# Layer 0's attention scores: tiles of one head and 128 queries, with high and low parts stacked in 128 rows

## The chip, the core and the metric

The kernel runs on one core of one Trainium2 chip. The metric is device time in microseconds (us), the median of several executions. The engines named below are TensorE (PE; its weight loads are shown as PEld), VectorE (DVE), ScalarE (ACT), GpSimd (POOL) and SyncE (SP), which here only issues DMAs.

## The reference, cut to what matters

Two layers over 256 tokens of width 1024. Layer 0 mixes tokens by dilated causal window attention, layer 1 by gated linear attention, each followed by a gated convolutional feed-forward block; all are modulated by the conditioning vector. The change is in layer 0 alone:

```python
A_CONFIGS = ((128, 1), (512, 4), (2048, 16))      # window, dilation: three groups
A_HEADS = 16;  A_HEAD_DIM = 64

s = jnp.einsum('bnqrhe,bnkrhe->bnrhqk', qb, kk) + bias      # per group
s = jnp.where(mask, s, NEG_INF)
m = jnp.max(s, axis=-1, keepdims=True);  p = jnp.exp(s - m);  den = jnp.sum(p, axis=-1)
o = einsum(p, v) / den;  lse = m + log(den)
...
wts = jax.nn.softmax(jnp.stack(lses), axis=0)               # over the three groups
o = jnp.sum(wts[..., None] * jnp.stack(outs), axis=0)
```

Mixing three softmaxes by the softmax of their log-sums is one softmax over the keys of all three groups together, with the group's own bias. The kernel computes it so.

## The kernel before, in words

**Precision.** A product of two float32 matrices is made of three passes in a fast float32 form (`fp32r`): each operand is split into a high part and a low remainder, and `mm3` (L196) multiplies high by high, low by high and high by low (L199, L200, L201). The casts to the high part run on ACT (L172), the subtractions for the low part on DVE (L178).

**Pairs.** Layer 0's 16 heads go in 8 pairs `u` = 0 to 7, two heads of 64 columns each. The loop is at L626. For each pair the queries and keys of the three groups `g` = 0, 1, 2 are projected (48 matmuls for each g, `pqk`), and then the values of all groups (`pv`, 48 matmuls of 384 columns). Pair 0, and the queries and keys of pair 1, come from one wide weight load (`w0`); from pair 2 on each g has its own load of 1 MB (`wqk`) and the values have two loads of 768 KB (`wv`). Loads go through 4 buffers (`raw`), split weights through 3 buffers for high parts (`whi`) and 3 for low ones (`wlo`). Between them DVE works off 96 dot products for the modulation (`ada`, L140).

**From the projection to the scores.** `evacuate` (L576) takes queries and keys out of the accumulator bank. For g = 0, whose scores need the three passes, it makes high and low parts: per head an ACT multiplication for the high part (L586) and a DVE operation for the low part (L587), then one ACT copy for the key's high part (L591) and one DVE subtraction for its low part. For g = 1, 2 it is one ACT and one DVE operation (L581) in plain float32.

**Scores.** There are four score tiles per pair, `r` = 0 to 3, of 128 rows: row 0 to 63 is the first head, 64 to 127 the second, and tile r holds the 64 queries whose token number leaves the remainder r when divided by 4. `shared` (L482) makes the 256 to 260 columns of group 0 in three 128-row matmuls on queries padded with zeros, so that the two heads don't mix; `dilated` (L488) adds two blocks of 64 columns for groups 1 and 2 with matmuls of 64 rows by 64 columns in plain float32, which the chip runs in two passes each (two records). Then, by tile: DVE adds the bias and takes the row maximum in one instruction (L510), ACT takes the exponential and its row sum (L529), DVE divides (L521, L522) and PE transposes (`turn`, L536: three 128-column transposes a tile, `t`; the copies of `t` to `pt` on ACT for even r and on DVE for odd r, L546). `outputs` (L550) multiplies with the values in matmuls of 128 rows by 64 columns (L557, L561), and ACT and DVE split the result (L568, L569).

**Order.** A scheduler orders the instructions of each engine before the run; in each engine's queue that order is fixed. `behind(...)` puts an instruction after others in that order. The scores of pair u stand after its values; the transposes of pair u-1 stand inside the projection of g = 1 of pair u (the call at L671 ahead of its last twelve matmuls, the call at L678 behind them), and the outputs of pair u-1 follow the scores of pair u. From pair 3 on the copies of `t` stand behind the last evacuation (`evacuated`, L545).

**Banks.** The accumulator has 8 banks: 2 with tag `p` (queries and keys of a g, and the values, in turn), 3 with tag `s` (scores), 3 with tag `t` (transposes, outputs, one score tile). The fourth transposed tile of a pair takes the `t` bank of the first one, so it waits for the ACT copy of that one. The projection of g = 2 takes the `p` bank of g = 0.

**Bias.** `load_bias` (L364) fetches, per pair, a tile of 128 rows by 387 columns in four small DMAs (two per head) on SP's queue, from rows that the kernel computed at its start; the tile has two buffers.

Of the kernel before, what the change touches and what calls it, by code (L numbers as in the profile page):

```python
# [11 lines left out]
F32 = mybir.dt.float32  # L12
# [45 lines left out]
def trunk(ctx: ExitStack, tc: tile.TileContext, I, out):  # L58
# [202 lines left out]
    def grouped(ap):  # L261
        return ap.rearrange("p (r i) -> p r i", r=4)
# [100 lines left out]

    def load_bias(u):  # L364

        b = att.tile([P, KEYS + 3], F32, tag="bias", name="bias")
        r = rows_d[:, :]
        for hh in range(2):  # L370
            own, at = slice(CH * hh, CH * hh + CH), r.offset + (2 * u + hh) * NROW
            nc.sync.dma_start(b[own, 2 * CH :], bass.AP(r.tensor, at, [[4, CH], [1, T + 3]]))
            nc.sync.dma_start(b[own, 0 : 2 * CH].rearrange("p (g x) -> p g x", g=2),
                              bass.AP(r.tensor, at + 512, [[1, CH], [P, 2], [1, CH]]))
        return b[:, :]


    sq = wspl.tile([P, 2048], F32, tag="wlo", name="sq").rearrange("p (k t) -> p k t", k=KT)
# [97 lines left out]
    def scores(u, q, k, v, bias):  # L476


        m = tmp.tile([P, 16], F32, tag="m", name="m")
        prob = [att.tile([P, KEYS + 3], F32, tag="prob", name="prob", bufs=4) for _ in range(4)]  # L480

        def shared(s, r):  # L482
            n = T + r + r % 2
            for i, (a, b) in enumerate(((0, 0), (1, 0), (0, 1))):
                last = mm(s[:, 0:n], q[0][a][:, r].rearrange("p a b -> p (a b)"), k[0][b][:, 0:n], start=(i == 0), stop=(i == 2))
            return last

        def dilated(s, r):  # L488
            own = slice(CH * r, CH * r + CH)
            for g in (1, 2):  # L490
                at = T + r + CH * (g - 1)
                for hh in range(2):
                    e = slice(E * hh, E * hh + E)
                    last = mm(s[e, at : at + CH], q[g][e, own], k[g][e, own], start=True, stop=True)
            return last

        for tiles in ((0, 1, 2), (3,)) if u == 0 else (range(4),):
            s = {r: bank("s", "t" if r == 3 and u else "s") for r in tiles}  # L500
# [4 lines left out]
            for r in tiles:  # L505
                with behind(last):
                    last = last_s[0] = dilated(s[r], r)
            for r in tiles:
                back = bass.AP(bias.tensor, bias.offset + KEYS - 1 + r, [bias.ap[0], [-1, KEYS + r]])
                nc.vector.tensor_tensor_reduce(  # L510
                    prob[r][:, 0 : KEYS + r], s[r][:, 0 : KEYS + r], back,
                    op0=ALU.add, op1=ALU.max, scale=1.0, scalar=-3e38, accum_out=m[:, r : r + 1],
                )
        pn = []

        def normalised():

            r = len(pn)
            f = m[:, 12 + r : 13 + r]
            pn.append(att.tile([P, KEYS], F32, tag="pn", name="pn", bufs=4))  # L520
            nc.vector.tensor_scalar(grouped(pn[r][:, 0:T]), by_residue(prob[r][:, 0:T]), f, None, op0=ALU.mult)  # L521
            norms.append(nc.vector.tensor_scalar(pn[r][:, T:KEYS], prob[r][:, T + r : KEYS + r], f, None, op0=ALU.mult))  # L522

        for hh in range(2):
            rs = slice(2 * hh, 2 * hh + 2)
            nc.vector.tensor_scalar(m[:, 4:8][:, rs], m[:, 0:4][:, rs], -1.0, None, op0=ALU.mult)
            for r in (2 * hh, 2 * hh + 1):
                c = prob[r][:, 0 : KEYS + r]
# [21 lines left out]
    def outputs(u, of, pt, *after):  # L550
        v = of[0]
        heads = [slice(E * hh, E * hh + E) for hh in range(2)]
        po = bank("po", "t")
        with behind(*after):
            for n in range(2):
                for hh, e in enumerate(heads):
                    mm(grouped(po[e, :T]), v[n][:, e], pt[:, :, P * n + E * hh : P * n + E * hh + E], start=(n == 0), stop=False)  # L557
            for r in range(4):
                for hh, e in enumerate(heads):
                    at = P * (r % 2) + P + E * hh  # L560
                    last_po[0] = mm(po[e, CH * r : CH * r + CH], v[r // 2][:, at : at + E],  # L561
                       pt[:, r, T + E * hh : T + E * hh + E], start=False, stop=(r == 3))
# [6 lines left out]
        nc.vector.tensor_tensor(lv, src, hv.bitcast(F32), op=ALU.subtract)  # L569
        o_hi.append(hi)  # L570
        o_lo.append(lo)
# [4 lines left out]
    def evacuate(q, k, g, pq, pk):  # L576

        if g:  # L580
            evacuated[:] = nc.scalar.mul(q[g], pq, 0.125), nc.vector.tensor_copy(k[g], pk)  # L581
            return evacuated[1]
        qh, ql = q[0]
        for hh in range(2):
            own = slice(E * hh, E * hh + E)
            nc.scalar.mul(qh[own, :, hh, :], grouped(pq[own]), 0.125)  # L586
            nc.vector.scalar_tensor_tensor(ql[own, :, hh, :], grouped(pq[own]), 0.125, qh[own, :, hh, :].bitcast(F32),  # L587
                                           op0=ALU.mult, op1=ALU.subtract)
        pk = in_order(pk)
        kh, kl = (as_tokens(z[:, 0:T]) for z in k[0])  # L590
        evacuated[:] = nc.scalar.copy(kh, pk), nc.vector.tensor_tensor(kl, pk, kh.bitcast(F32), op=ALU.subtract)  # L591
        return evacuated[1]

    def by_group(v, pv, n):

# [13 lines left out]
    for i in range(2):  # L609
        q_pair.append([])  # L610
        for j in range(2):
            at, n = ((112, 2 * T + 112), (0, 2 * T + 16))[j] if i == 0 else (0, 2 * T)
            z = att.tile([P, n], F32R, tag=f"q0{i}{j}", name="q", bufs=1)
            nc.gpsimd.memset(z.bitcast(F32), 0.0)
            q_pair[i].append(z[:, at : at + 2 * T].rearrange("p (r h c) -> p r h c", r=4, h=2))
            if i == 0:
                for s in range(2):
                    level[s].append(z[:, at + T * s : at + T * s + T])
# [5 lines left out]
                    nc.scalar.copy(a, b)  # L624

    for u in range(NPAIR):  # L626
        with tc.issue_after(last_load[0].ins):
            bias = load_bias(u)
        place = u % 2 if u < 4 else 1
        if u == 0:  # L630
            k_hi, k_lo = ([att.tile([P, T + 4], F32R, tag=f"k0{i}{j}", name="k", bufs=1) for j in range(2)] for i in range(2))
            for z in k_hi + k_lo:
                nc.gpsimd.memset(z[:, T:].bitcast(F32), 0.0)
        q, k = [q_pair[place]], [[k_hi[place], k_lo[place]]]
# [661 lines left out]
```

## Time and profile before

| | us |
|---|---|
| three runs | 770.27, 770.59, 772.97 |
| median | 770.59 |
| the profiled execution, first to last instruction (span) | 767.7 |
| layer 0's attention within it, about 48 to 276 | 228 |

The profile has no whole time of its own for the profiled execution; what lies around its span is taken from the runs (770.59 - 767.7 = 2.9). A row of the timeline reads: start in us from the first instruction, duration, engine, line of the kernel, operation, result <- operands, rows*columns of the array for PE, shape, and the number of merged instructions; in brackets how long the engine was idle before, and what ended that. A merged row's duration runs from the start of its first instruction to the end of its last one.

### The profile page before, as it was taken

To read this page: it belongs to the slowest core of one execution; us is meant where nothing else is said; L and a number is where in the kernel's file an instruction comes from. 1 tells how busy PE (TensorE), PEld (TensorE's weight loads), DVE (VectorE), ACT (ScalarE), POOL (GpSimd) and SP (SyncE) were. 2 spreads that over 40 slices of the span, in tenths; PEclk is the share of its full clock that TensorE was granted. 3 is DMA by queue.
4 is the path that set the end of the run, shared out by engine and by line. 5 is a ranking of instruction groups with operands and counts; after the bars stand their busy time and mean duration, and the time that the engine had idled before them with its cause. 6 is when DMAs were issued, how large, how long until landed. Compare 5 with 4: busy or idle time off the path is not lost.

```text
span 767.7 us, 15963 instructions
## 1 busy us (share of the span) xinstructions
PE 759.3 (99%) x6430; PEld 739.0 (96%) x6430; DVE 640.6 (83%) x1160; ACT 485.5 (63%) x949; POOL 13.2 (2%) x28
## 2 busy tenths in 40 slices
PE   8999999999999999999999999999999999999997
PEld 6999999999999999999999998899999999999996
DVE  6998988888888869999999778797668899998552
ACT  6477566465646568776767556745767866666552
POOL 1000000000000010000000000000010000000100
PEclk9999999999999999999999999999999999999999
DMA  8989778787787347878646975875355777644531
GB/s 346 402 298 408 269 244 278 255 277 261 278 275 245 112 146 279 333 239 272 235 139 234 353 277 202 328 257 189 131 192 196 251 267 256 239 151 152 192 110 56
DMA packets 35208, 184.72 MB, mean 241 GB/s; under 512 B 6140, under 2 KB 7676, under 8 KB 21182
## 3 DMA queue, kind: packets, MB, share of 16 engines
q1 hardware_dynamic: 34752, 183.26, 67.7%
q8 instruction: 50, 0.82, 0.4%
q10 hardware_dynamic: 382, 0.45, 0.2%
q14 instruction: 24, 0.20, 0.1%
HBM read 182.59 MB, written 1.10 MB: 239 GB/s over the span
## 4 chain that ended last, share of the span: by engine, by line
PE 93%; DMA 3%; ACT 2%; DVE 2%; issue 0%; ACTq 0%
PE pab L200 10%; PE pab L199 10%; PE pab L201 10%; PE pqk L199 5%; PE pqk L201 5%; PE pqk L200 5%; PE pd L200 5%; PE pd L199 5%; PE pd L201 5%; PE pv L200 3%; PE pv L199 3%; PE pv L201 3%; DMA raw<-in_w 2%; PE py L199 2%; PE py L201 2%; PE py L200 2%
## 5 line engine op out<-in xcount | busy, mean ns | idle before, releaser
L172 ACT CAST whi<-raw 128x1024 fp32r<-128x1024 f32 (+4 forms) x270 | 243.7, 946 | 104.0 <-PE pab L200 37.2
L178 DVE TENSOR_TENSOR wlo<-raw,whi 128x1024 fp32r<-128x1024 f32 (+3 forms) x254 | 270.5, 1091 | 44.0 <-ACT whi L172 43.3
L200 PE MATMUL pab<-hlo,whi 128*128 128x256 f32 x672 | 184.6, 276 | 0.0
L201 PE MATMUL pab<-hhi,wlo 128*128 128x256 f32 x672 | 184.6, 276 | 0.0
L199 PE MATMUL pab<-hhi,whi 128*128 128x256 f32 x672 | 183.2, 277 | 0.0
L200 PEld LDWEIGHTS pab<-hlo,whi 128*128 128x128 f32 x672 | 126.0, 188 | 0.2
L201 PEld LDWEIGHTS pab<-hhi,wlo 128*128 128x128 f32 x672 | 126.1, 188 | 0.0
L199 PEld LDWEIGHTS pab<-hhi,whi 128*128 128x128 f32 x672 | 125.1, 188 | 0.1
L140 DVE CUSTOM_DVE_ANT_0 ada_raw<-ada_raw,c_bc 128x1024 f32<-128x1024 f32 x96 | 113.0, 1218 | 5.7 <-DMA ada_raw<-in_w_ada 4.2
L199 PE MATMUL pqk<-hhi,whi 128*128 128x256 f32 x356 | 98.0, 281 | 0.0
L200 PE MATMUL pqk<-hlo,whi 128*128 128x256 f32 x356 | 97.4, 279 | 0.0
L201 PE MATMUL pd<-ghi,wlo 128*128 128x256 f32 x352 | 96.9, 276 | 0.0
L200 PE MATMUL pd<-glo,whi 128*128 128x256 f32 x352 | 96.9, 276 | 0.0
L199 PE MATMUL pd<-ghi,whi 128*128 128x256 f32 x352 | 96.8, 276 | 0.0
L201 PE MATMUL pqk<-hhi,wlo 128*128 128x256 f32 x356 | 96.7, 279 | 0.0
L199 PEld LDWEIGHTS pqk<-hhi,whi 128*128 128x128 f32 x356 | 66.5, 188 | 0.2
L200 PEld LDWEIGHTS pqk<-hlo,whi 128*128 128x128 f32 x356 | 66.7, 188 | 0.0
L201 PEld LDWEIGHTS pqk<-hhi,wlo 128*128 128x128 f32 x356 | 65.9, 188 | 0.7 <-issue 0.7
L200 PEld LDWEIGHTS pd<-glo,whi 128*128 128x128 f32 x352 | 66.0, 188 | 0.0
L201 PEld LDWEIGHTS pd<-ghi,wlo 128*128 128x128 f32 x352 | 66.0, 188 | 0.0
L199 PEld LDWEIGHTS pd<-ghi,whi 128*128 128x128 f32 x352 | 65.9, 188 | 0.0
L852 ACT ACTIVATE r<-pab,small 128x256 f32<-128x256 f32 x86 | 47.4, 559 | 7.3 <-DVE r L855 6.9
(248 smaller groups left out, 1408.8 us busy)
## 6 DMA issues: line engine op xcount, KB each, us to landing
raw<-in_w_up SPq DMA_DIRECT2D x42, 1024.0 KB, 4.9
ada_raw<-in_w_ada SPq DMA_DIRECT2D x29, 1024.0 KB, 5.9
raw<-in_w_down SPq DMA_DIRECT2D x32, 704.0 KB, 4.1
ada_raw<-in_w_ada SPq DMA_DIRECT2D x38, 512.0 KB, 6.4
raw<-in_wqk SPq DMA_DIRECT2D x18, 1024.0 KB, 5.9
raw<-in_wv SPq DMA_DIRECT2D x14, 768.0 KB, 5.9
raw<-in_w SPq DMA_DIRECT2D x7, 960.0 KB, 6.4
raw<-in_w_out_a SPq DMA_DIRECT2D x4, 1024.0 KB, 6.6
```

Of the source, the lines that this page charges most:

```text
L140: i = nc.vector.tensor_tensor_reduce(w, w, c_bc, op0=ALU.mult, op1=ALU.add, scale=1.0, scalar=0.0, accum_out=dot,)
L172: copied[0] = nc.scalar.copy(hi[:, c], raw[:, c])
L178: last_lo[0] = nc.vector.tensor_tensor(lo[:, c], raw[:, c], hi[:, c].bitcast(F32), op=ALU.subtract)
L199: mm(ps, a[0], b[0], start=start, stop=False)
L200: mm(ps, a[0], b[1], start=False, stop=False)
L201: return mm(ps, a[1], b[0], start=False, stop=stop)
L852: nc.scalar.activation(r, u[:, :T], AF.Identity, scale=cw[2], bias=col(C_CB + 44 * l + f))
```

## The change

The score tile is turned: tile `i` holds 128 queries of one head (head i % 2, half i // 2 of the queries in the order by remainder) in place of 64 queries of each of two heads.

- `qs` stacks the high part of one head's queries over their low part (64 + 64 rows), `ks` holds the key's high part of one head twice, one above the other. So one 128-row matmul gives high by high plus low by high (`shared`), and the third product, high by low, is a matmul of 64 rows by 128 columns (`rest_of`) from the head's own half of the rows.
- `dilated` loops over both halves and both groups, and then over the four (row half, column half) quarters of the array in the order (0,0), (1,1), (0,1), (1,0).
- `evacuate` for g = 0 writes `ks` with four ACT copies of 64 rows by 256 columns, after the old high and low parts of the key; `evacuated`, behind which the copies of `t` stand, now holds the last of them.
- The bias is by head: two tiles of 386 columns, four DMAs each, with one buffer each (pair 0's lie in a `pt` buffer). From pair 2 on they are issued after the first load of the pair's values instead of at the pair's start.
- The scores of a pair from pair 2 on stand behind the last matmul of its values; before, the first tile's could come earlier.
- `outputs` reads `pt` by head in two blocks of 128 columns instead of four of 64; its counts are the same.
- POOL's zero fills shrink to the padding.

```diff
@@ load_bias
-        b = att.tile([P, KEYS + 3], F32, tag="bias", name="bias")
+        both = []
         r = rows_d[:, :]
+        first = None if u else att.tile([P, 4, KEYS], F32, tag="pt", name="bias")
         for hh in range(2):
-            own, at = slice(CH * hh, CH * hh + CH), r.offset + (2 * u + hh) * NROW
-            nc.sync.dma_start(b[own, 2 * CH :], bass.AP(r.tensor, at, [[4, CH], [1, T + 3]]))
-            nc.sync.dma_start(b[own, 0 : 2 * CH].rearrange(...), bass.AP(r.tensor, at + 512, [[1, CH], [P, 2], [1, CH]]))
-        return b[:, :]
+            b = (first[:, 2 * hh : 2 * hh + 2, :].rearrange("p a b -> p (a b)")[:, 0 : KEYS + 2] if u == 0
+                 else att.tile([P, KEYS + 2], F32, tag=f"bias{hh}", name="bias", bufs=1)[:, :])
+            at = r.offset + (2 * u + hh) * NROW
+            for x in range(2):
+                own = slice(CH * x, CH * x + CH)
+                nc.sync.dma_start(b[own, 2 * CH :], bass.AP(r.tensor, at + x, [[4, CH], [1, T + 2]]))
+                nc.sync.dma_start(b[own, 0 : 2 * CH].rearrange(...), bass.AP(r.tensor, at + 512, ...))
+            both.append(b)
+        return both
@@ scores
-        def shared(s, r):
-            n = T + r + r % 2
-            for i, (a, b) in enumerate(((0, 0), (1, 0), (0, 1))):
-                last = mm(s[:, 0:n], q[0][a][:, r].rearrange("p a b -> p (a b)"), k[0][b][:, 0:n], start=(i == 0), stop=(i == 2))
-            return last
+        def shared(s, i):
+            hh, n = i % 2, width(i)
+            return mm(s[:, 0:n], qs[:, hh, P * (i // 2) : P * (i // 2) + P], ks[:, T * hh : T * hh + n], start=True, stop=False)
+        def rest_of(s, i):
+            hh, n = i % 2, width(i)
+            e = slice(E * hh, E * hh + E)
+            return mm(s[:, 0:n], qs[e, hh, P * (i // 2) : P * (i // 2) + P], kl[e, 0:n], start=False, stop=True)
-        def dilated(s, r):
-            own = slice(CH * r, CH * r + CH)
-            for g in (1, 2):
-                at = T + r + CH * (g - 1)
-                for hh in range(2):
-                    e = slice(E * hh, E * hh + E)
-                    last = mm(s[e, at : at + CH], q[g][e, own], k[g][e, own], start=True, stop=True)
-            return last
+        def dilated(s, tiles):
+            for half in range(2):
+                for g in (1, 2):
+                    for hh, x in ((0, 0), (1, 1), (0, 1), (1, 0)):
+                        i = 2 * half + hh
+                        if i in tiles:
+                            e, own = slice(E * hh, E * hh + E), slice(CH * (2 * half + x), CH * (2 * half + x) + CH)
+                            at = width(i) + CH * (g - 1)
+                            last = mm(s[i][CH * x : CH * x + CH, at : at + CH], q[g][e, own], k[g][e, own], start=True, stop=True)
+            return last
-                with behind(*(last_pv if r else last_t if u > 2 else [])):
-                    last = shared(s[r], r)
-            for r in tiles:
-                with behind(last):
-                    last = last_s[0] = dilated(s[r], r)
+            for half in range(2):
+                own = [i for i in tiles if i // 2 == half]
+                for i in own:
+                    with behind(*(last_pv if i or u > 1 else [])):
+                        last = shared(s[i], i)
+                for i in own:
+                    with behind(last):
+                        last = rest_of(s[i], i)
+            with behind(last):
+                last_s[0] = dilated(s, tiles)
@@ evacuate, g == 0
-        qh, ql = q[0]
-        for hh in range(2):
-            own = slice(E * hh, E * hh + E)
-            nc.scalar.mul(qh[own, :, hh, :], grouped(pq[own]), 0.125)
-            nc.vector.scalar_tensor_tensor(ql[own, :, hh, :], grouped(pq[own]), 0.125, qh[own, :, hh, :].bitcast(F32), ...)
-        pk = in_order(pk)
-        kh, kl = (as_tokens(z[:, 0:T]) for z in k[0])
-        evacuated[:] = nc.scalar.copy(kh, pk), nc.vector.tensor_tensor(kl, pk, kh.bitcast(F32), op=ALU.subtract)
-        return evacuated[1]
+        qs, (ks, kl, kh) = q[0], k[0]
+        k[0] = ks, kl
+        heads = [slice(E * hh, E * hh + E) for hh in range(2)]
+        for hh, own in enumerate(heads):
+            nc.scalar.mul(qs[own, hh, :], pq[own], 0.125)
+            nc.vector.scalar_tensor_tensor(qs[heads[1 - hh], hh, :], pq[own], 0.125, qs[own, hh, :].bitcast(F32), ...)
+        nc.scalar.copy(as_tokens(kh[:, 0:T]), in_order(pk))
+        low = nc.vector.tensor_tensor(as_tokens(kl[:, 0:T]), in_order(pk), as_tokens(kh[:, 0:T]).bitcast(F32), op=ALU.subtract)
+        for hh, own in enumerate(heads):
+            for to in heads:
+                high = nc.scalar.copy(as_tokens(ks[to, T * hh : T * hh + T]), in_order(pk[own]))
+        evacuated[:] = high, low
+        return low
@@ the loop over pairs
-        with tc.issue_after(last_load[0].ins):
-            bias = load_bias(u)
+        if u < 2:
+            with tc.issue_after(last_load[0].ins):
+                bias = load_bias(u)
...
+                if u > 1 and half == 0:
+                    with tc.issue_after(last_load[0].ins):
+                        bias = load_bias(u)
```

In `outputs`, the two matmuls now read `pt[:, hh::2, P * n : P * n + P]` and `pt[:, 2 * (r // 2) + hh, T + CH * (r % 2) : ...]`.

More of the change, by code (lines that the diff above doesn't have):

```diff
@@ L495, in dilated @@
             return last
         for tiles in ((0, 1, 2), (3,)) if u == 0 else (range(4),):
-            s = {r: bank("s", "t" if r == 3 and u else "s") for r in tiles}
-            for r in tiles:
-                with behind(*(last_pv if r else last_t if u > 2 else [])):
-                    last = shared(s[r], r)
-            for r in tiles:
-                with behind(last):
-                    last = last_s[0] = dilated(s[r], r)
-            for r in tiles:
-                back = bass.AP(bias.tensor, bias.offset + KEYS - 1 + r, [bias.ap[0], [-1, KEYS + r]])
+            s = {i: bank("s", "t" if i == 3 and u else "s") for i in tiles}
@@ new lines, in scores @@
+            for half in range(2):
[8 more added lines that the diff above has]
+                last_s[0] = dilated(s, tiles)
+            for i in tiles:
+                n = KEYS + 2 * (i // 2)
+                b = bias[i % 2]
+                back = bass.AP(b.tensor, b.offset + n - 1, [b.ap[0], [-1, n]])
@@ L510, in scores @@
                 nc.vector.tensor_tensor_reduce(
-                    prob[r][:, 0 : KEYS + r], s[r][:, 0 : KEYS + r], back,
-                    op0=ALU.add, op1=ALU.max, scale=1.0, scalar=-3e38, accum_out=m[:, r : r + 1],
+                    prob[i][:, 0:n], s[i][:, 0:n], back,
+                    op0=ALU.add, op1=ALU.max, scale=1.0, scalar=-3e38, accum_out=m[:, i : i + 1],
                 )
@@ L527, in scores @@
             for r in (2 * hh, 2 * hh + 1):
-                c = prob[r][:, 0 : KEYS + r]
+                c = prob[r][:, 0 : KEYS + width(r) - T]
                 exps.append(nc.scalar.activation(c, c, AF.Exp, bias=m[:, 4 + r : 5 + r], accum_out=m[:, 8 + r : 9 + r]))
@@ L561, in outputs @@
                     last_po[0] = mm(po[e, CH * r : CH * r + CH], v[r // 2][:, at : at + E],
-                       pt[:, r, T + E * hh : T + E * hh + E], start=False, stop=(r == 3))
+                       pt[:, 2 * (r // 2) + hh, T + CH * (r % 2) : T + CH * (r % 2) + CH], start=False, stop=(r == 3))
         if u == 0:
@@ L626, in trunk @@
     for u in range(NPAIR):
-        with tc.issue_after(last_load[0].ins):
-            bias = load_bias(u)
+        if u < 2:
+            with tc.issue_after(last_load[0].ins):
+                bias = load_bias(u)
         place = u % 2 if u < 4 else 1
         if u == 0:
-            k_hi, k_lo = ([att.tile([P, T + 4], F32R, tag=f"k0{i}{j}", name="k", bufs=1) for j in range(2)] for i in range(2))
-            for z in k_hi + k_lo:
+            k_hi, k_lo = ([att.tile([P, T + 4 * (i or j)], F32R, tag=f"k0{i}{j}", name="k", bufs=1) for j in range(2)] for i in range(2))
+            for z in k_lo:
                 nc.gpsimd.memset(z[:, T:].bitcast(F32), 0.0)
-        q, k = [q_pair[place]], [[k_hi[place], k_lo[place]]]
+        q, k = [q_pair[place][0]], [(q_pair[place][1], k_lo[place], k_hi[place])]
         for g in (1, 2):
```

20 lines of the change are left out of this document (12 added, 8 removed).

## The prediction

> **What bounds the kernel now.** First the page: the span and the busy shares.
>
> ```profile
> span 767.7 us, 15963 instructions
> ...
> PE 759.3 (99%) x6430; PEld 739.0 (96%) x6430; DVE 640.6 (83%) x1160; ACT 485.5 (63%) x949; POOL 13.2 (2%) x28
> ```
>
> PE is busy to 99%, its weight loads beside it to 96%; ACT has 37% free. As the share is a mean over stages, the next view is the busy time by stretch, for layer 0's attention alone (stretch, its length, then PE, PEld, DVE, ACT, POOL with counts, granted clock, DMA share, GB/s).
>
> ```profile
> 48.00:276.00 228.00, 227.90 (x2053) 222.50 (x2052) 194.03 (x398) 137.21 (x310) 0.00 (x0) 1.00 0.73 254
> ```
>
> PE never idles in these 228 us, at full clock; DVE is at 85%, ACT at 60%, the DMA engines at 73%. In the list of waits of this stretch no row has PE as the one that waits. So a microsecond taken from PE is worth a microsecond, as long as nothing that feeds PE comes later than now. The change takes from PE and gives to ACT and to SP's queue; the two halves of the question are how much PE saves, and how much room the feeders have.
>
> **PE's part.** One pair's scores and outputs in the timeline, PE alone:
>
> ```profile
> 252.81 1.24 PE L485 MATMUL s<-k,q 128*128 128x258 f32 x9
> 253.98 1.15 PE L494 MATMUL s<-k,q 64*64 64x64 f32 x32
> 255.06 1.08 PE L557 MATMUL po<-pt,v 128*64 128x256 f32 x8
> 255.97 0.64 PE L561 MATMUL po<-pt,v 128*64 128x64 f32 x16
> 256.53 0.39 PE L199 MATMUL py<-q,whi 128*128 128x256 f32 x1
> 256.76 0.28 PE L200 MATMUL py<-q,whi 128*128 128x256 f32 x1
> ```
>
> Matmuls overlap, so the cost of one is the distance to the next start. Nine shared matmuls run 1.24, the last of them 0.28: (1.24 - 0.28) / 8 = 0.12 each. The dilated ones are 32 records with the last 0.22 long: the last starts at 254.91, so 32 records need 0.93, in 16 steps of two records at 0.058 (one per head, in two different quarters of the array).
>
> The changes of shape cost as well. From the last shared start (252.81 + 8 x 0.12 = 253.77) to the first 64x64 record are 0.21 in place of 0.12, and from the last 64x64 start (254.91) to the outputs 0.15 in place of 0.06: each change costs 0.09. Behind it the first weight load isn't hidden: 256.53 to 256.76 is 0.23 in place of 0.12, so 0.105 more for 128 columns, and about 0.05 for 64 columns. Whether 64 rows by 128 columns, which the change adds, behaves so too, a place in layer 1 shows:
>
> ```profile
> 507.11 0.28 PE L200 MATMUL pqk<-hlo,whi 128*128 128x256 f32 x1
> 507.32 0.48 PE L1040 MATMUL kv<-v,kdT 64*128 64x256 f32 x1
> 507.32 0.48 PE L1040 MATMUL kdt<-v,kdT 64*128 64x256 f32 x1
> 507.64 0.38 PE L1040 MATMUL kv<-v,kdT 64*128 64x256 f32 x1
> ```
>
> 507.11 to 507.32 is 0.21 again. The two records that start at 507.32 use the two halves of the rows and start together; the next pass follows after 0.32, which is its own 0.21 and the 0.105.
>
> Now the count, from the order of PE's instructions in the changed kernel as built. (a) 96 shared matmuls become 32: -64 x 0.12 = -7.7. (b) 32 matmuls of 64 rows come, in 17 blocks of one or two side by side, at 0.11 a block (a shared one less its few ns of overlap): +1.9. (c) The dilated steps fall from 128 to 70, if four quarters run at once: -58 x 0.058 = -3.4. Only two at once are seen here, on the diagonal in the scores, and in the outputs two column halves on the same rows, two row halves above. Both kinds of neighbour run together, so I take four; the other end is 0. (d) Changes of shape rise from 28 to 60. Besides 17 entries to 64x128, there are 11 more returns to the full array, one more entry to the 64x64 shape, three more to the outputs' shape, since those are now cut in two in three places: 32 x 0.09 + 28 x 0.105 + 4 x 0.05 = +6.0. Sum -3.2: about -0.6 in each of pairs 3 to 7, -0.4 in pairs 0 to 2 together, +0.3 at the last outputs. Entering and leaving the new shape twice a pair eats nearly all that the fewer passes bring; what remains is the quarters.
>
> [...]
>
> **ACT's part, pairs 4 to 7.** Per pair ACT gets four more copies of 64 rows by 256 columns, 32 in all. They are not spread: in ACT's order they stand between the key's high part and the copy of the first transposed tile, and the first of them waits for the key's low part on DVE, which reads the same bank. What hangs on that copy: the fourth transposed tile takes the first one's `t` bank, and behind it on PE stands g = 2, and everything else. Pair 6, PE:
>
> ```profile
> 207.58 0.82 PE L544 MATMUL t<-ident,pn 128*128 128x128 f32 x6
> 208.16 0.48 PE L485 MATMUL s<-k,q 128*128 128x256 f32 x2
> 208.48 0.28 PE L199 MATMUL pqk<-q,whi 128*128 128x256 f32 x1
> ```
>
> ACT, the same stretch:
>
> ```profile
> 205.45 0.38 ACT L586 ACTIVATE q<-pqk 64x256 fp32r<-64x256 f32 x1 [1.92 <-DVE q L587]
> 206.32 0.37 ACT L591 CAST k<-pqk 128x256 fp32r<-128x256 f32 x1 [0.49 <-DVE q L587]
> 206.59 0.49 ACT L546 COPY pt<-t 128x384 f32<-128x384 f32 x1
> ```
>
> DVE:
>
> ```profile
> 198.75 0.41 DVE L569 TENSOR_TENSOR olo<-po,ohi 128x256 fp32r<-128x256 f32 x1
> ...
> 205.86 0.43 DVE L587 SCALAR_TENSOR_TENSOR q<-pqk,q 64x256 fp32r<-64x256 f32 x1 [0.45 <-ACT q L586]
> 206.73 0.42 DVE L591 TENSOR_TENSOR k<-pqk,k 128x256 fp32r<-128x256 f32 x1 [0.44 <-ACT k L591]
> ```
>
> Before, the copy ends at 207.08 and the fourth tile starts three transposes after 207.58, at 207.91: 0.8 of room. After: the low part ends at 207.15, then four copies. Two such evacuations in a row:
>
> ```profile
> 57.59 0.78 ACT L586 ACTIVATE q<-pqk 64x256 fp32r<-64x256 f32 x2
> ```
>
> 0.78 for two with 0.38 for the second: 0.40 apart. The bounds are 0.27 apart (206.32 to 206.59, two different banks) and 0.40; I take 0.38, the copy's length. 207.2 + 4 x 0.38 = 208.7, and 0.49 for the copy: 209.2. The built order also puts the first negation of the maxima ahead of DVE's 0.41 operation at 198.75, so this chain of maxima, exponentials, quotients and low parts starts about 0.3 earlier: 208.9. The fourth tile then starts 1.0 late. g = 2 starts 0.3 behind it, at 209.2 against 208.48, since the 0.32 of score work that stood between are gone: +0.7; another early score matmul (0.12) behind g = 2 is gone too: +0.6 a pair. That replaces PE's gain of 0.6 in the scores before, because the chain starts from the values' matmuls and runs on DVE and ACT, whatever PE saves meanwhile. Four pairs: +2.4. Ends: -2.4 (the copy holds nobody, PE's gain stays) and +4.4 (0.40 apart, nothing earlier).
>
> **Pair 3.** Here the built order of ACT is worse: evacuation of g = 1 and the cast of the second half of the values' load come ahead of the four copies. Before:
>
> ```profile
> 116.61 0.83 ACT L172 CAST whi<-raw 128x768 fp32r<-128x768 f32 x1 [0.47 <-ACT pt L546]
> 117.35 0.38 ACT L581 ACTIVATE q<-pqk 128x256 f32<-128x256 f32 x1
> 117.62 0.83 ACT L172 CAST whi<-raw 128x768 fp32r<-128x768 f32 x1
> ```
>
> ```profile
> 116.48 0.82 PE L544 MATMUL t<-ident,pn 128*128 128x128 f32 x6
> 117.06 0.48 PE L485 MATMUL s<-k,q 128*128 128x256 f32 x2
> 117.38 0.28 PE L199 MATMUL pqk<-q,whi 128*128 128x256 f32 x1
> ```
>
> g = 1 ends at 116.48 = T. After: first cast half T + 0.13, g = 1's query T + 0.9, second half T + 1.1, the four copies T + 1.9 to T + 3.4, the transposed tile to T + 3.8; the fourth transposes start there in place of T + 0.33, g = 2 at T + 4.2 in place of T + 0.9 (117.38). Less the 0.12: +3.2. Ends: 0 and +3.5.
>
> **The start.** The bias moves and doubles:
>
> ```profile
> L372 SPq DMA_DIRECT2D bias<-rows_d x16: 450/596/1350, 49.3 to 198.9; - x16
> ```
>
> Eight more DMAs ahead of pair 2's first load, at 0.6 each on SP: that load issues 5 later. Before, its first cast was where ACT waited for it:
>
> ```profile
> 60.25 1.05 ACT L172 CAST whi<-raw 128x1024 fp32r<-128x1024 f32 x1 [0.79 <-DMA raw<-in_wqk]
> ...
> 67.20 2.00 ACT L172 CAST whi<-raw 128x1024 fp32r<-128x1024 f32 x2
> ```
>
> After, the cast stands behind pair 1's first value copies, about where the second load's stood (67.20), so the DMA is there in time; but PE wants it at once:
>
> ```profile
> 67.83 0.28 PE L199 MATMUL pqk<-hhi,whi 128*128 128x256 f32 x1
> ```
>
> and the third matmul wants the low part, which on DVE now follows two maxima that wait for the score tiles:
>
> ```profile
> 67.02 0.56 DVE L510 CUSTOM_DVE_ANT_0 prob<-s,bias 128x384 f32<-128x384 f32 x1 [1.67 <-PE s L494]
> ```
>
> Walking the three built orders with the durations of before, PE waits 0.8 there, and g = 2 of pair 2 starts at about 86.9:
>
> ```profile
> 85.46 0.38 PE L199 MATMUL pqk<-hhi,whi 128*128 128x256 f32 x1
> ```
>
> against 85.46, which with PE's gain so far is a stall of 1.7. Then the keys of g = 1, whose bank the values need:
>
> ```profile
> 86.42 0.41 DVE L581 COPY k<-pqk 128x256 f32<-128x256 f32 x1
> ```
>
> now stand behind four maxima, dot products and two low parts, at about 92.9, 0.3 after g = 2 ends (86.9 + 48 x 0.12 = 92.6); g = 2's keys hold the second half of the values likewise. Together about +2.5. Ends: 0 and +5; this walk is my weakest. From pair 2 on the bias waits for the pair before and holds SP's later loads, ada pieces among them, by up to 5, eight DMAs per pair. I take 0:
>
> ```profile
> ACT whi L172 <- DMA raw<-in_wqk: 0.8, 1, 0.8
> ```
>
> is the only row of a weight load that ACT waited for, the one above; loads sit in four buffers well ahead. POOL's shorter fills are at the start, under other work: 0.
>
> **Sum.** Start +2.5, pair 3 +3.2, pairs 4 to 7 +2.4, and of PE's gains those that no chain swallows: -0.4 (pairs 0 to 2), -0.6 (pair 7), +0.3 (end). +7.4 on the span: 767.7 + 7.4 = 775.1; with the 2.9 that the runs' median lies above the span, **778.0**, 1.0% slower.
>
> **Rivals.** (1) Not slower: the copies hold nobody, because ACT runs them in overlap or the fourth tile isn't last at that place. Then only PE's sum of -3.2 and up to 2.5 of the start remain: 767.4 to 769.9. For it: ACT is idle 40% of the stretch. Against: the idle time isn't at that place; it decides from 0.8 of room upwards, and four copies in a row exceed that in every reckoning. (2) The quarters run two at a time: 0.46 a pair more wherever PE and not the chain is last (pairs 0 to 2 and 7, about 1.6): 779.6. For it, no run with four; against, the two kinds of pairs. (3) Pair 3 or the start doesn't stall, the rest does: 774.8 to 775.5, at the lower end 773. (4) The bias holds a weight load back past its use: one load late by 5 gives 783 and more.
>
> **Chances.** Forecast 0.56, (1) 0.17, (2) 0.13, (3) 0.09, (4) 0.05. The range of 770.5 to 783.5 leaves out most of (1) and (4). A measurement here can tell about 0.5% from no change, 3.9 us: faster than 766.7 needs (1) and a start that costs nothing, 0.04; within, the rest of (1) and the lower part of (3), 0.18; slower 0.78.
>
> **What would show it.** Right: PE's waits appear, `t` waiting for `pt` on ACT, once some 3 us in pair 3 and about 1 us in each of pairs 4 to 7; the dilated group of a pair 0.5 long for 32 records; about 0.3 from a pair of 64-row matmuls to the next shared one. Wrong: PE still at 228 busy in 228, or a wait on a weight load's DMA as the longest one. If the four copies start less than 0.3 apart, rival (1) gains.

## The result, and the profile after

| | before | after |
|---|---|---|
| time, median of four runs each | 770.43 us | 783.76 us |
| lowest to highest | 770.26 to 772.97 | 781.0 to 785.17 |
| ratio, 95% interval | | 1.0167 (1.0141 to 1.0192) |
| span of the profiled execution | 767.7 | 783.4 |

The kernel became 1.7% slower. The direction was forecast, the size was not: +7.4 was said, +13.3 came, 0.3 above the upper end of the range. First the page of the changed kernel.

```profile
span 783.4 us, 15976 instructions
...
PE 765.8 (98%) x6398; PEld 738.4 (94%) x6398; DVE 641.5 (82%) x1160; ACT 496.4 (63%) x981; POOL 11.3 (1%) x24
```

PE runs 32 matmul records fewer and is busy 6.5 us longer, and the span holds 17.6 us in which it isn't busy (before: 8.4). Busy time alone would have misled: it grows because matmuls follow each other more slowly, at the beginning (0.21 us from start to start in place of 0.11) and, at a granted clock of 0.50, at about 70 us and behind a wait, as will be seen. The waits of layer 0's attention (who waited for whom: us in total, times, longest):

```profile
PE t L562 <- ACT pt L564: 8.6, 5, 3.4
```

This row isn't in the list of before. It is the wait that the prediction named, five times, once for about 3 us. Pair 3 and pair 6 in the timeline, PE and then ACT:

```profile
122.80 0.49 PE L562 MATMUL t<-ident,pn 128*128 128x128 f32 x3
126.70 0.55 PE L562 MATMUL t<-ident,pn 128*128 128x128 f32 x3 [3.41 <-ACT pt L564]
127.00 0.36 PE L199 MATMUL pqk<-q,whi 128*128 128x256 f32 x1
...
220.24 0.49 PE L562 MATMUL t<-ident,pn 128*128 128x128 f32 x3
221.93 0.55 PE L562 MATMUL t<-ident,pn 128*128 128x128 f32 x3 [1.20 <-ACT pt L564]
222.23 0.36 PE L199 MATMUL pqk<-q,whi 128*128 128x256 f32 x1
```

```profile
122.92 0.83 ACT L172 CAST whi<-raw 128x768 fp32r<-128x768 f32 x1 [0.71 <-PE pqk L200]
123.66 0.38 ACT L599 ACTIVATE q<-pqk 128x256 f32<-128x256 f32 x1
123.94 0.82 ACT L172 CAST whi<-raw 128x768 fp32r<-128x768 f32 x1
124.66 1.50 ACT L612 CAST q<-pqk 64x256 fp32r<-64x256 f32 x4
126.17 0.86 ACT L564 COPY pt<-t 128x384 f32<-128x384 f32 x2
...
219.87 1.50 ACT L612 CAST q<-pqk 64x256 fp32r<-64x256 f32 x4 [0.49 <-DVE k L609]
221.40 0.48 ACT L564 COPY pt<-t 128x384 f32<-128x384 f32 x1
```

Four copies in 1.50 us, the transposed tile's copy right behind, and the fourth tile on PE within 0.1 of that copy's end. In pair 3 cast, query and cast come ahead of them, and with T = 122.80 the prediction's T + 3.8 and T + 4.2 are 126.6 and 127.0.

The wait has a second part. The stretches around it (PE, PEld, DVE, ACT, POOL busy with counts; granted clock; DMA share; GB/s):

```profile
124.00:126.00 2.00, 0.00 (x0) 0.00 (x0) 2.00 (x3) 1.96 (x6) 0.00 (x0) 1.00 0.82 236
126.00:128.00 2.00, 1.30 (x9) 1.30 (x10) 2.00 (x6) 1.76 (x7) 0.00 (x0) 0.83 0.90 299
128.00:130.00 2.00, 2.00 (x11) 2.00 (x11) 1.10 (x2) 0.00 (x0) 0.00 (x0) 0.50 0.96 265
130.00:132.00 2.00, 2.00 (x16) 2.00 (x15) 0.00 (x0) 0.00 (x0) 0.00 (x0) 0.81 0.99 383
```

Behind the wait PE gets half its clock (0.50) for 3.4 us, from 127.33 to 130.74: 11 matmuls in 2 us in place of 19. The 48 products of g = 2 take 7.15 from the first start to the last; before they took 5.41 (117.38 to 122.79). Nothing waits there, so the column of the granted clock is the only place where this loss is seen.

A pair's scores and outputs, pair 7:

```profile
268.07 0.39 PE L497 MATMUL s<-k,q 64*128 64x256 f32 x2
268.39 0.50 PE L492 MATMUL s<-q 128*128 128x258 f32 x2
268.82 0.39 PE L497 MATMUL s<-k,q 64*128 64x258 f32 x2
269.14 0.69 PE L507 MATMUL s<-k,q 64*64 64x64 f32 x32
269.76 1.08 PE L575 MATMUL po<-pt,v 128*64 128x256 f32 x8
```

The 32 dilated records start within 0.48 (the last is 0.22 long), and their single starts lie 7 ns apart in groups of four: the four quarters run at once. 268.07 to 268.39 is the 0.32 from a pair of 64-row matmuls to the next shared one.

The last reading is far from the change. The beginning, after:

```profile
7.93 1.06 PE L211 MATMUL ms<-sq,ones_d 128*128 128x256 f32 x2
10.20 1.22 PE L211 MATMUL ms<-sq,ones_d 128*128 128x256 f32 x2 [1.21 <-DVE sq L391]
...
15.30 2.93 PE L297 MATMUL warm<-ones_d 128*128 128x128 f32 x12
17.88 1.05 PE L675 MATMUL pqk<-hhi,whi 128*128 128x256 f32 x6
```

The first product starts at 17.88; before it started at 13.98, and when PE comes to the last products of pair 0's values, at 62.6 by the kernel before, 3.4 of this are left. It begins with 1 us of waiting for x's second half; after that all warm-up matmuls run 0.21 apart, not 0.11. The first runs below ask whether the change does this.

### The profile page after: what moved, and what is told of

Its sections match the earlier page's. It is cut to its first block, busy times and chain, and to the rows that moved or that the text cites. A ratio compares the mean times of both kernels' runs of the same rounds, so it can differ in the third digit from the quotient of the medians.

```text
span 783.4 us, 15976 instructions
## 1 busy us (share of the span) xinstructions
PE 765.8 (98%) x6398; PEld 738.4 (94%) x6398; DVE 641.5 (82%) x1160; ACT 496.4 (63%) x981; POOL 11.3 (1%) x24
## 4 chain that ended last, share of the span: by engine, by line
PE 96%; ACT 2%; DMA 1%; DVE 1%; issue 0%; ACTq 0%; DVEq 0%
PE pab L199 10%; PE pab L200 10%; PE pab L201 10%; PE pqk L199 6%; PE pqk L201 6%; PE pqk L200 6%; PE pd L199 5%; PE pd L200 5%; PE pd L201 5%; PE pv L200 3%; PE pv L199 3%; PE pv L201 3%; PE pqk L675 2%; PE py L199 2%; PE py L201 2%; PE py L200 2%
```

## The experiments

Each is the changed kernel with the edit shown, unless said otherwise.

**The same kernel again**

> The changed kernel once more, unaltered. In its first profile the second half of x landed 1.05 us later than before, the warm-up matmuls then ran at half clock to the end, and the first product started at 17.88 instead of 13.98 us. Theory (chance of that execution): the first product starts between 13 and 15 us again, as in four other kernels with the same beginning, the span is 779 to 781 and the median 780.5 to 783. Rival (the shorter fills on GpSimd or the changed order delay it each time): 17 to 18 us again, 783.8.

Measured: 782.15 us (780.47 to 783.64), ratio 1.0145 (1.0120 to 1.0171). The profiled execution took 780.47, span 778.7:

```profile
13.14 1.60 PE L297 MATMUL warm<-ones_d 128*128 128x128 f32 x12
14.50 0.95 PE L675 MATMUL pqk<-hhi,whi 128*128 128x256 f32 x6
```

The beginning of the first profile was chance: in the eleven other profiles below the first product starts between 13.2 and 15.0. So of the first profile's +15.7 on the span 11.0 are left in this one. Of the 4.7 between them 3.2 lie in the beginning and 1.0 in a stretch of half clock at about 70 us (granted 0.84 in 70 to 74 and 0.73 in 74 to 78) that this execution doesn't have (1.00 in both). This second profile is used for the account further down.

**The four copies on another engine**

```
-                high = nc.scalar.copy(as_tokens(ks[to, T * hh : T * hh + T]), in_order(pk[own]))
+                nc.gpsimd.tensor_copy(ks[to, T * hh : T * hh + T], kh[own, 0:T])
```

(`high` is then the copy of the key's high part.)

> The changed kernel with one edit: the four copies of the key's high part are made by GpSimd from the high part in SBUF, so that none stands in ScalarE's order and none reads the bank of the products; the transposed tile's copy is ordered behind the key's high part only. Theory (the four copies hold the fourth transposed tile in pairs 3 to 7): the five waits of t for pt go. Those were 3.58, 1.36, 1.36, 1.36 and 1.74 us, and about 1.4 us at a lower granted clock behind the first: 783.8 - 10.8 = 773.0, and between 771.5 and 775. Rival (the time goes at the start, before pair 3, or in PE's own shapes): the waits stay or others take their place, 780 to 784.

Measured: 772.55 (772.32 to 774.66), ratio 1.0044 (1.0029 to 1.0059). In the stretch of pairs 3 to 7 no row has t waiting for pt. From one turn of pairs 3 and 4 to the next 29.75 pass in place of 34.97, and 30.21 in place of 31.2 in pairs 4 to 6. The copies are the cause of most of what was lost: against the kernel before run beside each, 2.9 are left of 13.3, or of 11.8 in the second run. What is late next shows in the same list:

```profile
PE pv L199 <- DVE k L599: 1.0, 4, 0.5
```

Before, pairs 4 to 6 took 30.37 each and PE was the limit; PE's own work in a pair is now 0.6 to 0.7 less, but only 0.16 arrives.

**Each copy twice**

```
+                for _ in range(2):
+                    high = nc.scalar.copy(as_tokens(ks[to, T * hh : T * hh + T]), in_order(pk[own]))
```

> The changed kernel with each of the four copies of the key's high part made twice on ScalarE, so that eight stand where four stood. Theory: every copy lies on the path in pairs 3 to 7, four more at 0.375 us apart are 1.5 us a pair: the waits become 5.1, 2.9, 2.9, 2.9 and 3.2 us, +7.5, and somewhat more where the clock sinks behind a longer wait: 791 to 794. Rival (they are mostly covered, and the waits come from elsewhere): under +3, below 787.

Measured: 806.41 (805.54 to 808.14), ratio 1.0481 (1.0465 to 1.0497): +24 in place of +7.5. Both numbers were wrong. The order changed, and more than the tile waits; pair 4:

```profile
162.09 0.55 PE L562 MATMUL t<-ident,pn 128*128 128x128 f32 x3 [3.05 <-DVE pt L564]
163.90 0.58 PE L199 MATMUL pqk<-q,whi 128*128 128x256 f32 x1 [1.26 <-ACT q L613]
```

```profile
164.00:166.00 2.00, 2.00 (x10) 2.00 (x11) 0.56 (x2) 0.82 (x3) 0.00 (x0) 0.50 1.00 403
166.00:168.00 2.00, 2.00 (x11) 2.00 (x11) 0.00 (x0) 0.00 (x0) 0.00 (x0) 0.50 1.02 406
168.00:170.00 2.00, 2.00 (x12) 2.00 (x12) 0.00 (x0) 0.00 (x0) 0.00 (x0) 0.55 0.12 49
```

Pair 4 takes 37.3 in place of 31.2. Of the 6.1, 1.9 are the longer wait of the tile, about 1.5 the wait of g = 2 for the last copy, which still reads the bank, and 2.7 the clock: g = 2's products need 8.3 up to the values' first, not 5.6. As a test of 0.375 a copy the run is spoilt by the new order; what it shows is half clock behind these waits of 3.05 and 1.26 (0.50 in 164 to 168), which cost 2.7 us in this pair; over its whole span the mean granted clock is 0.976, in the first profile 0.995.

**Work in place of the wait**

```
+            if r == 3 and len(o_hi) == 2:
+                idle = bank("warm", "s")
+                with behind(last_t[0]):
+                    for _ in range(28):
+                        last_t[0] = mm(idle[:, :P], ones_d, ones_d, start=True, stop=True)
```

> The changed kernel with 28 matmuls of ones by ones, which nothing reads, ahead of the fourth transposed tile of pair 3, in PE's 3.6 us of waiting there. Theory (the clock sinks because PE stands idle, and that costs beside the wait itself): the tile starts as late as before, but the granted clock behind it stays 1.00 instead of 0.67 and 0.91, and the 1.3 to 1.6 us lost between the tile and the values' matmuls go: 782.3. Rival (the clock's fall isn't from that idle time): no change in what is lost behind, 783.8, or more by what the added matmuls delay.

Measured: 782.23 (781.08 to 783.39), ratio 1.0164 (1.0149 to 1.0179). The number agrees by accident: 28 of these matmuls are 56 records and last 6.15, so the tile came 2.7 later than it could. But the 48 products of g = 2 took 5.51 at a granted clock of 1.00. With half as many:

> As the run with 28 matmuls in pair 3's wait, but 14: the 28 were 56 records and took 6.15 us, so that they overran the wait of 3.58 by 2.6. 14 take 3.07 and end ahead of the tile. Theory (the clock sinks because PE stands idle): the wait's end stays, the 48 products of g = 2 behind it take 5.5 as they did behind the 28, not 7.15, so the kernel is 1.6 less than the changed kernel run beside it, at equal beginnings. Rival (it was the overrun, not the work, that kept the clock): 7.15 again, no difference.

Measured: 779.09 (778.28 to 780.65), ratio 1.0109 (1.0086 to 1.0132), 3.1 below the unaltered kernel beside it, more than the 1.6 expected, but the medians of both hold a beginning that varies. The stretch itself, from pair 3's turn to the end of its outputs, takes 23.51 in place of 25.11: 1.60 less.

```profile
120.24 3.29 PE L562 MATMUL warm<-ones_d 128*128 128x128 f32 x28
123.82 0.55 PE L567 MATMUL t<-ident,pn 128*128 128x128 f32 x3 [0.29 <-ACT pt L569]
124.12 0.36 PE L199 MATMUL pqk<-q,whi 128*128 128x256 f32 x1
```

```profile
123.00:125.00 2.00, 1.71 (x15) 1.52 (x15) 2.00 (x6) 1.88 (x7) 0.00 (x0) 1.00 0.85 262
125.00:127.00 2.00, 2.00 (x19) 2.00 (x18) 1.20 (x2) 0.00 (x0) 0.00 (x0) 1.00 0.80 213
```

The wait ends where it did, PE works through it for nothing, and the clock behind it stays at 1.00. So the loss behind the wait comes from PE standing idle: shown.

**The bias loads on another queue**

```
+        both, queue = [], nc.gpsimd if u < 2 else nc.sync
...
-                nc.sync.dma_start(b[own, 2 * CH :], ...
+                queue.dma_start(b[own, 2 * CH :], ...
```

> The changed kernel with the bias loads of pairs 0 and 1, sixteen DMAs, issued by GpSimd's queue instead of SyncE's. Theory (the start is late because they stand ahead of pair 2's first weight load): that load issues at about 51 instead of 61.5 us, its cast stands ahead of pair 1's value copies again, PE's waits of 0.5 and 0.26 us at 73 us go, and with them the stretch at a granted clock of 0.84 and 0.73 behind them: 2 to 3 us of the 2.95 that the start loses, 780.8 to 781.8. The order of ScalarE around pair 3 shifts with it, which can change the long wait there by up to 1.5 either way. Rival (the start loses by the scores' shapes mixed into other matmuls): under 1 us.

Measured: 780.10 (778.92 to 780.65), ratio 1.0136 (1.0119 to 1.0153). That is 2.0 below the second run of the changed kernel, with intervals that overlap, and its span is 0.9 shorter; what was gained isn't where the reason given has it. The first weight load of pair 2 did issue at 50.5, and its cast moved ahead; yet pair 3's turn starts at 118.50, where it started at 116.55. Other waits came in place of those that went:

```profile
84.12 0.55 PE L562 MATMUL t<-ident,pn 128*128 128x128 f32 x3 [2.50 <-DVE pt L564]
90.42 0.86 PE L575 MATMUL po<-pt,v 128*64 128x256 f32 x5 [0.65 <-DVE pt L564]
94.59 0.41 PE L562 MATMUL t<-ident,pn 128*128 128x128 f32 x2 [1.02 <-DVE pn L539]
```

The gain is pair 3's: one cast and the query of g = 1 no longer stand ahead of the four copies there, the tile waits 1.7 and the clock stays (0.999 over the span), 3.3 less. The run doesn't show SP's queue to be what makes the start late.

**Shapes grouped**

```
-            for half in range(2):
-                own = [i for i in tiles if i // 2 == half]
-                for i in own:
...
+            for i in tiles:
+                with behind(*(last_pv if i or u > 1 else [])):
+                    last = shared(s[i], i)
+            for i in tiles:
+                with behind(last):
+                    last = rest_of(s[i], i)
```

> The changed kernel with the four shared products of a pair ahead of its four remainders, where now two, two, two and two alternate: in pairs 3 to 7 one entry to the 64-row shape and one return fewer, 60 changes of shape become 43. By the profile after, rest to shared 0.313 and the next shared one 0.222 become plain 0.115 steps: 0.3 to 0.4 us less ahead of each pair's maxima. Theory 1 (the chain that holds the fourth tile starts at the end of the scores): that is gained in each pair though PE stands waiting there, -0.35 in five pairs and up to -1 in pairs 0 to 2: 2 to 3 us less than the changed kernel run beside it. Theory 2 (the chain starts at the values' last product, as the prediction had it): pairs 3 to 6 gain nothing, 0.3 to 1.3 less.

Measured: 781.27 (778.13 to 782.50), ratio 1.0128 (1.0097 to 1.0159), 0.9 below the unaltered kernel in medians, within the spread of both. The profile decides between the two theories:

```profile
185.35 0.55 PE L560 MATMUL t<-ident,pn 128*128 128x128 f32 x3 [1.60 <-ACT pt L562]
```

From the values' last product to the end of the outputs a pair takes 3.11 in place of 3.52, and the tile waits 0.40 longer (1.60 against 1.20). From turn to turn pairs 4 to 6 take 31.2 as before. Theory 2: what PE saves in the scores becomes waiting, as the prediction had it. In pair 7 the wait grew to 1.97, and this time the clock sank behind it (0.63 in 248 to 250, 0.51 in 250 to 252) and 1.5 were lost there (48 products in 7.04 in place of 5.50).

**The parts together, and what is late next**

The copies on GpSimd, the shapes grouped, all scores behind the values' last product in pairs 0 and 1 too (`behind(*last_pv)`), and the heads of the outputs' first products in the other order, so that the one whose tiles come last is first:

```
-                for hh, e in enumerate(heads):
+                for hh, e in reversed(list(enumerate(heads))):
                     mm(po[e, :T]...
```

> Three edits on the changed kernel: the four copies on GpSimd from SBUF, the four shared products ahead of the four remainders, and the outputs' first products with the head that is copied last coming first, so that the scheduler no longer puts other products between them; all scores of a pair behind the values' last product. 60 changes of shape become 38. Expected: 772.5 as with the copies alone, less 0.35 in up to five pairs, 0.7 at the last outputs, and 1 to 2 in pairs 0 to 2: 768 to 770, about the kernel before. Rival (the key copy of the second group, which held the values' first product by 0.45 a pair in the run with the copies on GpSimd, takes what PE saves): 771 to 772.5.

Measured: 770.56 (769.12 to 771.49), ratio 0.9998 (0.9986 to 1.0009): the kernel before again, in between theory and rival. The key copy of the second group now holds the values' first product, and behind the longest of these waits, in pair 2, the clock sinks:

```profile
PE pv L199 <- DVE k L597: 4.5, 5, 1.9
```

```profile
94.00:96.00 2.00, 2.00 (x9) 2.00 (x8) 1.80 (x7) 2.00 (x8) 0.00 (x0) 0.56 0.57 124
96.00:98.00 2.00, 2.00 (x9) 2.00 (x8) 2.00 (x6) 0.50 (x1) 0.00 (x0) 0.59 0.58 102
```

To that version one edit more, and to the kernel before the same edit alone:

```
-                for _ in range((3, 0, 3)[g]):
+                for _ in range((2, 1, 3)[g]):
```

> The version before (copies on GpSimd, shapes grouped, outputs in one piece), and one of the three dot products of VectorE that follow the first group's keys put behind the second group's. In the version before, the only long waits of PE from 57 to 290 us are the values' first product for the second group's keys, which VectorE copies behind three dot products of 1.35 to 1.4 us: 4.5 us in five pairs, the longest 1.9. Theory (that copy is what comes late next): with one dot product fewer ahead of it it comes 1.3 earlier, 0.4 to 0.9 a pair in pairs 3 to 6 go, and most of the longest: 766 to 768, faster than the kernel before. Rival (ScalarE's casts or the low parts are as late as that copy): 769.5 to 770.5.

> The kernel before, with the same shift of one dot product behind the second group's keys. There PE waits for nothing from 48 to 276 us, so the edit alone should bring nothing: 769.5 to 770.8. If it is faster than that, the last step of the version above owes nothing to the scores' new form.

Measured: 766.87 (766.49 to 768.58), ratio 0.9972 (0.9961 to 0.9983); the kernel before with the edit alone 769.72, ratio 1.0004 (0.9992 to 1.0016). The wait is down to

```profile
PE pv L199 <- DVE k L597: 1.3, 5, 0.4
```

and the turns of pairs 4 to 6 lie 29.87 apart. This is the fastest version found, 0.3% ahead of the kernel before and 2% ahead of the changed one; as the edit alone brings the kernel before nothing, the gain needs the rest of that version. The other order of the heads wasn't tried on the kernel before, so how much of the gain is the new form of the scores isn't shown. With two dot products moved, `(1, 2, 3)`:

> The same with two of the three dot products behind the second group's keys. If one was enough in pairs 3 to 7, this gives nothing more there; the wait of 1.9 in pair 2 may want both: 765.5 to 768. Rival (the dot products, now behind the second group's keys, hold the low parts of the values' weights): 769 or more.

Measured: 767.96 (766.62 to 770.77), ratio 0.9983 (0.9973 to 0.9993). The second one brings nothing; one wait of 1.5 in the start remains.

## Why the forecast held in direction and missed in size

The account by stretches, from the second profile of the changed kernel (span 778.7) against that of before. Stretches run from the first transposition of one turn to that of the next:

| stretch | forecast | measured |
|---|---|---|
| to the values of pair 0 (62.6 us) | 0 | +0.2 |
| start, up to pair 3's turn | +2.5 - 0.4 | +1.9 |
| pair 3 | +3.2 | +4.6 |
| pairs 4, 5, 6 | +0.6 each | +0.8 each |
| pair 7 | +0.6 - 0.6 | +1.4 |
| last turn to layer 0's next matmuls | +0.3 | +0.9 |
| after PE's last product | 0 | -0.5 |
| span | +7.4 | +11.0 |

The span's 11.0 and the measured rows agree to 0.1. From there to the median of 783.76 it is 3.3 more than that execution's 780.47: the beginning, and a sinking of the clock at about 70 us (0.84 and 0.73 in 70 to 78 of the first profile, 1.00 in the second), vary between executions, here by up to 4.7 us; single runs of the kernel before, too, reach 773.5, but most lie close to 770. The 2.9 that the forecast added to the span was 1.1 too much; each later profile's own time lies 1.8 above its span.

- *PE's sum of about -0.6 a pair*: right in pairs 3 to 7; for pairs 0 to 2 see the start. The scores and outputs of pair 7 end 0.24 earlier behind the values' last product, and the 0.44 of score work that stood elsewhere is gone: 0.68. The four quarters run at once, rival (2) fell. The price of 0.09 and 0.105 for a change of shape is seen in 268.07 to 268.39.
- *ACT's part, the chain*: right in mechanism and place, shown by taking the copies off ACT. The step "starts about 0.3 earlier" was too kind: it gave 0.2, so the tile came 1.13 late where 1.0 was said. That is part of the 0.2 a pair that were missing.
- *Pair 3, +3.2*: the wait was right to 0.1 (126.70 against 126.6). The term was mis-sized because PE's time behind the wait was reckoned at the old 0.113 a product: the clock sank (0.75 in 122 to 126 and 0.83 in 126 to 130 of the second profile) and added 1.6. No row of this stretch before could show it, as PE never waits there.
- *Pair 7, -0.6*: counted twice. The 0.44 was already in the 0.6 of the chain, so only 0.24 were left to subtract. Besides, its tile waited 0.38 longer than in pairs 4 to 6; the low part of its key came that much later. In pairs 4 to 6 the first negation of the maxima (L544) stands ahead of DVE's subtraction for the outputs, as the prediction read the built order; in pair 7 it stands behind it, and the chain has no head start. Pair 6, then pair 7:

```profile
211.65 0.16 DVE L544 TENSOR_SCALAR m<-m 128x2 f32<-128x2 f32 x1
211.72 0.41 DVE L587 TENSOR_TENSOR olo<-po,ohi 128x256 fp32r<-128x256 f32 x1
...
242.89 0.42 DVE L587 TENSOR_TENSOR olo<-po,ohi 128x256 fp32r<-128x256 f32 x1
243.22 0.23 DVE L544 TENSOR_SCALAR m<-m 128x2 f32<-128x2 f32 x2
```

- *The start, +2.5, "this walk is my weakest"*: the sum was near (1.9 against 2.1 with PE's share) by luck. Of the waits that the walk named only the first shows, where 0.8 was said: 0.61 from one start on PE to the next in place of 0.12, at about 70 us. Taking the bias loads off SP, whose queue the walk blamed, made the start later. The loss is PE's own: from the last products of pair 0's values to pair 3's turn PE changes its shape 26 times, before 11 times. From start to start these 26 steps take 6.4 us and those 11 took 1.9; all other steps together, that wait among them, take 2.6 less. So PE's share, put at -0.4, came out at about +1.4. In the version with all parts 16 changes take 3.6, and pair 3's turn still comes at 117.08, behind a wait of 1.9 and a clock of 0.56 and 0.59; with the one dot product moved it comes at 114.23 (before: 114.41).
- *The last outputs, +0.3*: 0.9. The scheduler put 16 other products between the first two of 24 output products and the rest, two changes of shape more than were costed in full. With the heads in the other order they stay together.
- *Rival (1)*, that the copies hold nobody, fell; *rival (4)*: no weight load came late. *Rival (3)* neither: pair 3 stalled, and the start lost its time in PE's shapes.

What failed are sizes: in pair 3 a wait was priced at its length, without the 1.6 of half clock behind it; in pair 7 a saving was counted twice and a head start counted that isn't there; and in the start PE's changes of shape were priced too low, which stalls that didn't come made up for by luck.

## What to carry to other kernels

Four copies a pair, which fill 1.5 us of an engine with 37% to spare, cost 9 to 10 us in all here, because they stand in its order ahead of the one copy that PE's next buffer hangs on. Look at what the queue holds there, not at the engine's share. Price a wait on PE at its length, and read the granted clock behind it: where it sank to half here, that cost 1.5 us (shapes grouped, pair 7) to 2.7 us (each copy twice, pair 4) more, and useless matmuls in pair 3's wait won that part back, 1.60 us. When the bound is taken away, the next one may stand close behind: of PE's 0.6 to 0.7 us a pair 0.16 arrived with the copies off ACT, and 0.50 only with the dot product moved as well.

## What the runs showed of the hardware that was not expected

- **The clock behind a wait.** By the distances between starts on PE, the gap of 3.7 in pair 3 was followed by half clock (0.50 in 128 to 130 of the first profile), and so was that of 3.3 in pair 4 with doubled copies (0.50 in 164 to 168). Two of 2.2 were too (shapes grouped, pair 7: 0.63 and 0.51 in 248 to 252; the parts together, pair 2: 0.56 and 0.59 in 94 to 98); one of 2.77 in the run with the bias on GpSimd's queue was not (1.00 in 82 to 88), and neither were the four from 1.46 to 1.85 in pairs 4 to 7 of the first profile. That profile's trace records the granted clock itself: full from 18.10, 0.50 for 3.41 us from 72.72 and again from 127.33. The two falls come 16 and 32 times 3.413 us behind 18.10. Cut into such steps from 18.10 on, PE is idle for 2.78 us in the one that ends with the fall at 127.33, and for 1.58 us at most in any other up to PE's last product. The fall at 72.72 doesn't fit: in the step ahead of it PE is idle for 0.01 us. Of the four profiles whose order is the changed kernel's up to there, three have a fall at about 70 us (the first; 28 useless matmuls: 0.58 and 0.56 in 70 to 74; 14 of them: 0.57 there), and the second profile of the changed kernel has none (1.00). Why stays open.
- **GpSimd beside VectorE.** Four copies of 64 rows by 256 on GpSimd take 1.76 at 60.33, 0.44 each, and 4.46 at 178.15, beside dot products on VectorE; the 19 copies from 119 to 250 take 1.10 on the mean:

```profile
60.33 1.76 POOL L612 CAST q<-k 64x256 fp32r<-64x256 f32 x4 [58.90 <-ACT k L608]
...
178.15 4.46 POOL L612 CAST q<-k 64x256 fp32r<-64x256 f32 x4 [25.75 <-ACT k L608]
```

```profile
178.47 1.21 DVE L140 CUSTOM_DVE_ANT_0 ada_raw<-ada_raw,c_bc 128x1024 f32<-128x1024 f32 x1
...
179.60 1.41 DVE L140 CUSTOM_DVE_ANT_0 ada_raw<-ada_raw,c_bc 128x1024 f32<-128x1024 f32 x1
```

Two of the three dot products ahead of the second group's keys grew from 1.21 to 1.41; without copies on GpSimd, in the changed kernel, the 24 from 119 to 250 take 1.22 on the mean. That these 0.4 are most of the 0.5 by which those keys hold the values is argued, not tested.
